# Three order changes at the seams of a two-phase float16 MLP: where eight transposing reads are issued, two gelus behind two takes, and one maximum's transpose behind a first product

## The chip, the cores and the metric

The kernel runs on one core of a Trainium2 chip. Its engines each work through a queue of their own in order: TensorE (PE, matmuls), VectorE (DVE), ScalarE (ACT), GpSimd (POOL) and SyncE (SP, which here only issues transfers). The metric is the device time of the whole program in microseconds (us). Times are medians of several runs; a profile is one execution of its own.

## The reference

Inputs are x (8 x 1024 x 1024), w1 (1024 x 4096) and w2 (4096 x 1024), all float32.

```python
h = x @ w1
h = 0.5 * h * (1 + np.tanh(np.sqrt(2 / np.pi) * (h + 0.044715 * h ** 3)))
return (h @ w2).astype(np.float32)
```

## The kernel before, in words

**Two phases.** The 8192 rows of x are cut into 32 pairs of 128-row blocks. Phase one computes gelu(x @ w1) and stores it as float16 in a DRAM tile `gd` of each pair; phase two reads `gd` back transposed and multiplies it by w2. Values are scaled into float16 by maxima that are found on the way, and both phases save matmuls by forming sums of blocks, in the manner of Strassen.

**Phase one** goes by quads. A quad `(k, r)` is pair k with quarter r of each half of the columns of w1: 256 rows, 2 x 512 columns. Class `Quad1` makes its four output blocks with seven products of four matmuls (128 x 512), in three PSUM banks: `pa` (3 buffers), `pb` (2), `pc` (3). `order` lists 128 quads (`NQ`): the first six pairs (`FIRST`) by quarters, the 22 middle pairs one by one, and the last four (`LAST`) by quarters again. The first seven quads are done plainly; from quad 7 on, `unit(u)` writes out one quad's work interleaved with what is left of quads u-1 and u-2: on PE `m1(u)`, `m7(u-1)`, `m3(u-2)`, `m2(u)`, `m6(u)`, `m5(u)`, `m4(u-1)`.

A finished block goes through ACT (a copy out of PSUM into a tile `e`, lines 503, 513, 522, and the gelu, line 454), POOL (the cast to `g`, line 177) and SP (the store to `gd`, line 459). There are 8 tiles `g`; four are written in each quad, so a cast of quad u needs the stores of two quads earlier to have landed. The stores are collected in `held` and let go at two places in each unit, always leaving the last two for the next place. Tiles `e` are freed by POOL's cast; they share a pool of 11 with the float16 sums `gs` of phase two.

**Slots.** Side work is entered into `todo` by `plan(u, slot, f, ...)` and written out by `background(u, slot)`, 0 to 6, between the products of unit u. Three kinds matter here:

- `widest_w1(r)` and `scale_w1(r)` find the largest absolute value of a quarter of w1. DVE reduces each partition and writes the result along the rows of `spread` (line 155); PE transposes `spread` into `rows` (line 162, in `all_partitions`); DVE reduces that (line 165) and derives the scales that `factors` and the casts of w1 use.
- `fetch_w2` (line 396) brings one of 25 prepared combinations of w2, 512 KB, from the DRAM tile `wd`, seven to a quarter: in quads 117 and 118, 121 and 122, 125 and 126, and four in unit 128. They use the tiles that w1's finished quarters leave.
- `load_g(k, i)` (line 550) is one transposing read of a quarter of a pair's `gd`, 512 KB, issued by SP.

**Where the phases meet.** Units 128 and 129 have no quad of their own. They finish quads 126 and 127, and twice each call `extra`, which is `second(3)`: three products of phase two. Phase two has 26 products (`PRODUCTS`) of eight matmuls (128 x 256) for each pair; each adds into the bank of one of its chains, and after a product `take` reads the bank into output blocks `o`: the first take of a block is ACT's (line 575), the later ones DVE's (line 571). A chain's next product waits until the takes of its last one have read the bank. `sum_g` (lines 168 and 171, DVE) makes the combinations of the pair's transposed blocks. Pairs 0 and 1 are read during phase one, eight reads in all; from pair 2 on four reads are issued together at the start of the pair before.

In unit 128 ACT's queue holds, in this order: the copy of `m7(127)`, quad 126's `g21` (a gelu in place in PSUM and a cast by ACT itself, line 175), the gelu `g11`, takes of products 0, 1 and 2, the gelus `g22(127)` and `g12(126)`, takes of products 3 and 5.

Of the kernel before, what the change touches and what calls it, by code (L numbers as in the profile page):

```python
# [79 lines left out]
def kernel(  # L80
# [380 lines left out]
    def let_go(n=None):  # L461
        for f in held[:n]:
            f()
        del held[:n]
# [157 lines left out]
    NQ = len(order)  # L622
    todo = {}

    def plan(u, slot, f, *args):
        assert 0 <= u, (f, args)
        todo.setdefault((u, slot), []).append((f, args))

    def background(u, slot):
        for f, args in todo.pop((u, slot), ()):  # L630
            f(*args)
# [37 lines left out]
    for r in range(2, NR):  # L669
        u = (r - 1) * FIRST - 1  # L670
        for n in range(8):
            v = u - 1 + n // 2
            if r == 2:
                plan(*((4, 1), (5, 0), (5, 2), (6, 1))[n // 2], load_w1, r, n)
                look = ((5, 3), (5, 4), (6, 1), (7, 1), (7, 1), (7, 4), (7, 5), (8, 1))[n]
                plan(*look, look_w1, r, n, S if n % 2 else V)
            else:
                plan(v, 1, load_w1, r, n)
                look = (v + 2, 1) if n == 1 else (v + 1, 3 + n % 2)
                plan(*look, look_w1, r, n, S if n == 1 else V)  # L680
        plan(u + 3, 3 if r == 2 else 5, widest_w1, r)
        plan(*((u + 3, 6) if r == 2 else (u + 4, 2)), scale_w1, r)
        plan(u + 4, 2, factors, 0, FIRST, r)
        for n in range(8):
            v, slot = ((4, 3), (4, 4), (4, 5), (5, 1), (4, 3), (4, 5), (5, 3), (4, 6))[n]
            plan(u + v, slot, cast_w1, r, n, (G, S, G, S, G, V, S, V)[n])
        for i, t in enumerate((T1, T3, T2, T4)):
            plan(u + 5 + i // 2, (4, 6, 1, 3)[i], sum_w1, r, t)
# [21 lines left out]
    u = at[middle[0]] - 1  # L710
# [8 lines left out]
    for c in range(8):  # L719
        v = u + 2 + c * 7  # L720
# [12 lines left out]
    for i, node in enumerate(FORMS):  # L733
        r, n = divmod(i, 7)
        plan(at[last[0]] + (r + 1) * LAST + (r < 3) + (n > 4), n, fetch_w2, node)
    for i in range(4):
        plan(NQ - 10 + i, 3, load_g, 0, i)
        plan(NQ - 5 + i, 3, load_g, 1, i)
    for at_, *what in LEFT_SUMS:
        if at_ < 0:  # L740
            plan(NQ - 1, 6, sum_g, 0, *what)
# [1 line left out]
    def unit(u, extra):  # L743
        q = now.get(u)
        p1, p2 = now.get(u - 1), now.pop(u - 2, None)
        if u < NQ:
            q = now[u] = Quad1(*order[u])
            q.m1()
        background(u, 0)
        if p1:  # L750
            p1.m7()
        if p2:
            p2.g21(u >= NQ)
        if p1:
            p1.g11()
        if u >= NQ:
            extra()
        let_go(len(held) - 2 if len(held) > 2 else 0)
        background(u, 1)
        if p2:  # L760
            p2.m3()
        background(u, 2)
        if u < NQ:
            q.m2()
        background(u, 3)
        if u < NQ:
            q.m6()
        if p1:
            p1.g22()
        if p2:  # L770
            p2.g12()
        let_go(len(held) - 2 if len(held) > 2 else 0)
        background(u, 4)
        if u < NQ:
            q.m5()
        background(u, 5)
        if p1:
            p1.m4()
        if u >= NQ:
            extra()  # L780
        background(u, 6)

    with tc.manual_schedule(
# [76 lines left out]
        for u in range(FIRST + 1, NQ):  # L860
            unit(u, None)
# [4 lines left out]
        for u in range(NQ, NQ + 2):  # L866
            unit(u, lambda: second(3))
# [34 lines left out]
```

## Time and profile before

| | us |
|---|---|
| median of 3 runs | 1540.9 (1540.29 to 1543.32) |
| the profiled execution, whole | 1538.59 |
| its span, first to last instruction | 1536.8 |
| PE busy in the span | 1520.7 (99%) |
| DVE, ACT, POOL busy | 1181.2, 734.6, 479.2 |
| mean granted TensorE clock | 0.999 |

The page's first part gives the busy time of each engine. The second cuts the span into 40 slices; PE shows a 7 in the first and a 9 (90% or more) in all others. In the list of groups the matmuls of phase one stand as 379 ns each (128 x 512) and those of phase two as 273 ns (128 x 256); they overlap in the pipeline, and their starts are what counts. In the timeline a quad of phase one is 28 matmuls and repeats every 6.04 us, and a pair of phase two is 208 matmuls and repeats every 22.71 us. An answer row of the timeline reads: start, duration, engine, line, operation, output and inputs, count, and in brackets the idle time before it and what ended it.

### The profile page before, as it was taken

Reading aid. Unit: us, or ns where it says so; the run is one execution under the profiler, and the core shown is the slowest. Engines: PE = TensorE matmul, PEld = TensorE weight load, DVE = VectorE, ACT = ScalarE, POOL = GpSimd, SP = SyncE. Lnnn points to the kernel's source line nnn. Section 1 sums busy time; section 2 is a strip of 40 time slices with the busy share of each in tenths; the row PEclk is TensorE's granted clock in tenths of the full one; section 3 lists DMA queues with packets and bytes.
Section 4 is the critical chain, followed back from the end, with each engine's and each line's share of the span. In section 5 each row is a group of like instructions: output and inputs, shape, how many; then the busy total and the mean of one; then the engine's idle time right before and its main releaser. Section 6 shows DMA issues by size and latency. Waiting matters only on the chain.

```text
span 1536.8 us, 28616 instructions
## 1 busy us (share of the span) xinstructions
PE 1520.7 (99%) x10398; PEld 1014.6 (66%) x10398; DVE 1181.2 (77%) x2409; ACT 734.6 (48%) x1302; POOL 479.2 (31%) x592
## 2 busy tenths in 40 slices
PE   7999999999999999999999999999999999999999
PEld 4444444444444444444448888888888888888888
DVE  6896788777877777574348888888888888888886
ACT  7778777777777777787662111111111111111111
POOL 5778554555666655554440000000000000000000
PEclk9999999999999999999999999999999999999999
DMA  9754988878788787873997668767767867866772
GB/s 351 238 189 126 299 273 292 253 233 243 211 239 269 220 260 229 246 201 103 268 258 193 132 128 154 140 134 140 148 131 135 155 136 123 165 135 124 154 141 80
DMA packets 459807, 293.94 MB, mean 191 GB/s; under 512 B 333840, under 2 KB 427024, under 8 KB 459664
## 3 DMA queue, kind: packets, MB, share of 16 engines
q1 hardware_dynamic: 456208, 279.52, 71.4%
q0 software_dynamic: 3456, 12.58, 2.6%
q8 instruction: 81, 1.33, 0.4%
q14 instruction: 62, 0.51, 0.1%
HBM read 96.99 MB, written 114.29 MB: 137 GB/s over the span
## 4 chain that ended last, share of the span: by engine, by line
PE 95%; DMA 1%; POOL 1%; ACT 1%; issue 1%; DVE 1%; SPq 0%; ACTq 0%; POOLq 0%
PE pa L402 51%; PE pc L402 30%; PE pb L402 14%; POOL g L177 1%; DMA gd<-g 1%; DMA wn<-in_w_dram 0%; ACT e L442 0%; PE pb L414 0%; POOL wn L276 0%; DMA xn<-in_x_dram 0%; ACT junk L190 0%; PE turned L216 0%; POOL w L177 0%; DVE x L179 0%; ACT xT L221 0%
## 5 line engine op out<-in xcount | busy, mean ns | idle before, releaser
L402 PEld LDWEIGHTS <-gs 128*128 128x128 f16 x4608 | 451.2, 98 | 56.4 <-issue 3.4
L177 POOL TENSOR_SCALAR g<-e,rs 128x512 f16<-128x512 f32 x446 | 364.6, 827 | 286.1 <-ACT e L454 250.0
L402 PEld LDWEIGHTS <-xs 128*128 128x128 f16 x1936 | 189.4, 98 | 227.9
L168 DVE TENSOR_TENSOR e<-pc,e 128x512 f32<-128x512 f32 x242 | 161.7, 686 | 199.9 <-ACT e L522 198.3
L402 PEld LDWEIGHTS <-xT 128*128 128x128 f16 x1676 | 163.2, 98 | 196.8 <-issue 1.7
L402 PE MATMUL pa<-w,gs 128*128 128x256 f16 x2304 | 289.0, 273 | 3.1 <-ACT o L575 3.1
L402 PE MATMUL pa<-w,xT 128*128 128x512 f16 x1080 | 256.1, 379 | 1.2 <-DVE w L179 0.9
L454 ACT ACTIVATE e<-e,us 128x512 f32<-128x512 f32 x363 | 249.2, 719 | 3.2 <-DVE e L168 3.2
L402 PE MATMUL pa<-w,xs 128*128 128x512 f16 x968 | 248.4, 379 | 0.0
L402 PE MATMUL pc<-w,xs 128*128 128x512 f16 x968 | 248.4, 379 | 0.0
L402 PEld LDWEIGHTS <-gT 128*128 128x128 f16 x2048 | 200.7, 98 | 23.6
L575 ACT ACTIVATE o<-pa,vo 128x256 f32<-128x256 f32 x96 | 45.3, 472 | 332.7 <-PE pa L402 332.7
L402 PE MATMUL pc<-w,gs 128*128 128x256 f16 x1536 | 193.8, 273 | 0.0
L402 PE MATMUL pa<-w,gT 128*128 128x256 f16 x1024 | 132.7, 273 | 0.0
L402 PE MATMUL pb<-w,xT 128*128 128x512 f16 x484 | 124.2, 379 | 0.0
L571 DVE SCALAR_TENSOR_TENSOR o<-pc,vo,o 128x256 f32<-128x256 f32 x160 | 77.1, 482 | 58.0 <-PE pc L402 58.0
L513 ACT COPY e<-pa 128x512 f32<-128x512 f32 x121 | 70.9, 586 | 91.7 <-PE pa L402 85.5
L171 DVE TENSOR_TENSOR gs<-gT,gs 128x1024 f16<-128x1024 f16 x160 | 109.3, 683 | 0.3 <-POOL g L177 0.3
L571 DVE SCALAR_TENSOR_TENSOR o<-pa,vo,o 128x256 f32<-128x256 f32 x192 | 92.3, 481 | 19.9 <-PE pa L402 19.9
L402 PE MATMUL pc<-w,gT 128*128 128x256 f16 x768 | 100.1, 274 | 0.0
L402 PE MATMUL pb<-w,gs 128*128 128x256 f16 x768 | 99.5, 273 | 0.0
L503 ACT COPY e<-pa 128x512 f32<-128x512 f32 x121 | 70.1, 579 | 50.8 <-PE pa L402 50.6
(104 smaller groups left out, 1444.8 us busy)
## 6 DMA issues: line engine op xcount, KB each, us to landing
gd<-g SPq DMA_DIRECT2D x484, 128.0 KB, 3.3
wn<-in_w_dram SPq DMA_DIRECT2D x72, 512.0 KB, 5.5
xn<-in_x_dram SPq DMA_DIRECT2D x64, 512.0 KB, 5.4
out_dram<-o SPq DMA_DIRECT2D x62, 512.0 KB, 3.5
w<-wd SPq DMA_DIRECT2D x25, 512.0 KB, 5.8
wn<-in_w_dram POOLq DMA_DIRECT2D x24, 512.0 KB, 5.9
wd<-wt SPq DMA_DIRECT2D x24, 512.0 KB, 5.0
gd<-g SPq DMA_DIRECT2D x14, 256.0 KB, 5.4
```

Of the source, the lines that this page charges most:

```text
L168: V.tensor_tensor(out=o, in0=a, in1=b, op=ALU.add)
L171: V.tensor_tensor(out=o, in0=a, in1=b, op=ALU.subtract)
L177: G.tensor_scalar(out=o, in0=i, scalar1=s, scalar2=1.0, op0=ALU.mult, op1=ALU.mult)
L402: nc.tensor.matmul(bank, lhsT=left(i), rhs=right[i], start=start and i == 0, stop=i == n - 1, skip_group_check=True,)
L454: S.activation(out=e, in_=src, func=ACT.Gelu_apprx_tanh, scale=self.u[half][s])
L503: S.copy(self.e11, self.pa)
L513: S.copy(self.e12, self.pa)
L571: V.scalar_tensor_tensor(out=o, in0=ps, scalar=v, in1=o, op0=ALU.mult, op1=ALU.add)
L575: S.activation(out=o, in_=ps, func=ACT.Copy, scale=v)
```

## The change

1. The eight transposing reads of pairs 0 and 1 move. Before, they are planned in slot 3 of units 118 to 121 and 123 to 126; after, in slot 3 of units 114, 115, 116, 119 (pair 0) and 120, 123, 124, 127 (pair 1).
2. In units 128 and 129, which have no quad of their own, the gelus `g22` and `g12` are written out at the end of the unit, behind the second call of `extra`, instead of between `m3` and `m4`. On ACT this moves two gelus (of quads 127 and 126) behind the takes of products 3 and 5; the order of DVE and PE is untouched by it.
3. `scale_w1` for quarter 2 of w1 moves from slot 6 of unit 8 to slot 0 of unit 9. On PE its one transpose stands behind the four matmuls of `m1` of quad 9 instead of ahead of them; on DVE its three small operations stand behind one more sum of x.

No operation is added or removed.

```diff
-        plan(*((u + 3, 6) if r == 2 else (u + 4, 2)), scale_w1, r)
+        plan(u + 4, 0 if r == 2 else 2, scale_w1, r)
...
-    for i in range(4):
-        plan(NQ - 10 + i, 3, load_g, 0, i)
-        plan(NQ - 5 + i, 3, load_g, 1, i)
+    for i, v in enumerate((14, 13, 12, 9, 8, 5, 4, 1)):
+        plan(NQ - v, 3, load_g, *divmod(i, 4))
...
-        if p1:
-            p1.g22()
-        if p2:
-            p2.g12()
+        def gelus():
+            if p1:
+                p1.g22()
+            if p2:
+                p2.g12()
+
+        if u < NQ:
+            gelus()
...
             p1.m4()
         if u >= NQ:
             extra()
+            gelus()
```

## The prediction, made before the changed kernel was run

> **What bounds the kernel now.** I read the page's first parts, then the waits with PE as the waiting engine, then the timeline at the places they name, then windows around them. PE is busy for 99% of the span, and outside the first 40 us only two waits lie on it:
>
> ```profile
> PE pa L402 <- ACT o L575: 3.1, 1, 3.1
> PE rows L162 <- DVE spread L155: 0.9, 1, 0.9
> ```
>
> Elsewhere phase one repeats every 6.04 us and phase two every 22.71 us, which is 28 and 208 matmul starts: nothing but these two gaps can be won, and any gain is a shift of all that follows. The windows around the first gap (busy time of PE, PEld, DVE, ACT, POOL, then granted clock, DMA share, GB/s):
>
> ```profile
> 797.79:803.86 6.07, 6.07 (x41) 3.92 (x40) 4.50 (x8) 2.36 (x4) 4.53 (x4) 1.00 1.04 226
> 803.86:807.13 3.27, 0.17 (x2) 0.00 (x1) 1.29 (x2) 1.72 (x4) 0.43 (x2) 0.90 1.02 225
> 807.13:810.36 3.23, 3.23 (x18) 2.33 (x18) 2.85 (x5) 2.37 (x5) 0.66 (x2) 0.58 0.99 353
> 810.36:833.07 22.71, 22.71 (x206) 19.99 (x205) 18.67 (x37) 5.07 (x10) 2.79 (x3) 1.00 0.49 179
> ```
>
> PE stands for 3.27 us, and behind that the granted clock is 0.58 for 3.23 us. Sixteen matmuls (products 3 and 4) start from 807.13 to 810.19, 3.06 us, where sixteen take 1.75 later. The gap thus costs 3.27 + 1.31 = 4.58 us. The chain that makes it, from the timeline:
>
> ```profile
> 789.24 6.28 SPq L550 DMA_TRANSPOSE gT<-gd  x1
> 795.61 1.00 SPq L459 DMA_DIRECT2D gd<-g  x2
> ...
> 798.17 4.00 SPq L550 DMA_TRANSPOSE gT<-gd  x1
> ...
> 802.27 1.01 SPq L459 DMA_DIRECT2D gd<-g  x2
> 805.41 0.69 ACT L175 ACTIVATE g<-pa,rs 128x512 f16<-128x512 f32 x1 [3.05 <-DMA gT<-gd]
> 806.00 0.71 ACT L454 ACTIVATE e<-e,us 128x512 f32<-128x512 f32 x1
> 806.61 0.46 ACT L575 ACTIVATE o<-pa,vo 128x256 f32<-128x256 f32 x1
> 807.13 1.86 PE L402 MATMUL pa<-w,gs 128*128 128x256 f16 x8 [3.10 <-ACT o L575]
> ```
>
> Backwards: product 3 waits for the take of product 0 (806.61), which stands on ACT behind a gelu and behind the cast at 805.41. That cast needs a tile `g`, freed when the store at 802.27 lands (3.1 us later). The store stood on SP behind a transposing read that holds the queue for 4.00 us. It belongs to slot 3 of quad 126, whose PE work began at 786.56; the cast it stores ran on POOL at 789.81. So SP is some 11 us late. The row names the read as releaser; the program's own wait is for the stores, and the first one's landing fits.
>
> Why it is late: in 741 to 801 the DMA share is 1.00 to 1.06 in every 12 us window (in 717 to 729 it is 0.26). The eight reads hold SP for 2.31 to 6.28 us, median 4.40. The two shortest (2.31, 2.45) follow four stores with no w2 fetch close before; the two longest (6.04, 6.28) follow three fetches directly.
>
> The second gap, in unit 8:
>
> ```profile
> 74.90 1.22 DVE L150 TENSOR_REDUCE w1c<-wn 128x1 f32<-128x1024 f32 x1 [0.66 <-DMA wn<-in_w_dram]
> ...
> 77.23 1.03 PE L402 MATMUL pa<-w,xT 128*128 128x512 f16 x4
> 78.77 0.29 DVE L155 TENSOR_SCALAR spread<-identity,w1a 128x128 f32<-128x128 f32 x1
> 79.11 0.33 PE L162 MATMUL rows<-identity,spread 128*128 128x128 f32 x1 [0.86 <-DVE spread L155]
> 79.28 1.03 PE L402 MATMUL pa<-w,xT 128*128 128x512 f16 x4
> ```
>
> The four matmuls of `m4` are through at 77.23 + 4 x 0.216 = 78.09; `m1` of quad 9 is ready but stands behind the transpose, which waits for `spread`, late by a transfer that landed at 74.88. The clock stays at 1.00 here.
>
> **The change, part by part.**
>
> *Transpose of quarter 2's maximum.* The DVE order up to `spread` is the same, so it is ready at 79.06 again. `m1` runs at 78.09 to 78.96, the transpose at 79.11, `m7` at 79.28 instead of 80.14: gain 0.86 us, the length of `m1`, with 0.15 of wait left. On DVE the maximum comes behind one more sum (0.41 us): scales ready at about 81.0 instead of 80.7. Their first readers run at 83.75 (`factors`) and 84.37 (POOL's cast, behind its own queue), so this is hidden by some 2.7 us; without that cover it would cost 0.4. Bounds 0.3 (the transfer lands earlier) to 0.86.
>
> *Reads moved.* Work of the DMA engines, from windows: 717 to 729 moves eight stores at share 0.26, so 0.39 us a store; a pair of phase two (four reads, two 512 KB outputs, about 0.65 of 22.7 us, the outputs 1.5 us each at the stores' rate) gives 2.9 us a read; 741 to 801 (about 14 fetches, 7.5 reads, 36 stores) leaves 1.86 us a fetch. Before, quads 117 up to the late store ask for 21 x 1.86 + 8 x 2.9 + 42 x 0.39 = 78.6 us, and took from 732.3 to about 805.4, 73.1: the estimate is 7% high. After, three of the reads lie in quads 114 to 116 where the share is 0.26; up to the same store of quad 126 there are 19 fetches, 4 reads, 40 stores: 62.5, scaled 58.2 us, from 732.3 that is 790.5, about when its cast is done. SP's own time agrees: in a quad with a read 4 stores (0.5 each) + 2.3 to 4.4 against 6.04; in one with five fetches (0.45 each) 4.3. So the store goes out near 790.5 to 791, not 802.3, and lands, at 3.3 to the longest 7.2 us seen there, by 798.2. ACT's cast would want it at 800.9: copy at 799.77 (end of `m7` 799.51 plus the 0.26 seen in every quad), gelu 0.48 later, cast 0.69 later. Gelu 801.5, take of product 0 at 802.1 to 802.6; product 3 may start at 803.86. Margin 1.2 us. The gap goes with its slow clock: gain 4.58.
>
> What is late next? The last read (quad 127) starts near 794.3, ends by 798.7 (4.4) or 800.6 (6.3), and holds the stores behind it; the first is wanted by ACT's cast of `g21(127)` in unit 129, at about 809. Even at 7.2 to landing it is there by 808.3. Behind that cast stands the take of product 7, wanted by product 12 at 812.6.
>
> DVE becomes the next tight one: the sum for product 6 (node 25) ends a row that starts at 800.9 (sums without a break from 797.0, then `vo` and `vn`, 0.8): 800.9 + 0.6 (add) + 3 x 0.65 (sums) + 0.4 (take) + 0.65 (add) + 1.4 (two sums) = 805.9, wanted at 806.48. Bounds for the reads: 1 us (a shorter gap with the slow clock left) to 4.58.
>
> *Gelus later.* In unit 128 as it now runs, both orders have the take of product 3 in time: with the gelus ahead, 803.9 (product 2's second take, behind DVE's) + 0.46 + 2 x 0.66 + 0.46 = 806.1 against 806.48; behind, 805.45. Value 0 here; it turns 0.4 us of cover into 1.0. Put behind, the gelus wait for product 5 (806.5 + 0.3) and end at 808.4; POOL's casts follow at 808.6 to 810, and DVE's next sum that needs a freed tile comes at 809.9. Bounds -0.5 to +0.5 if that sum waits, or if the cover would have been gone.
>
> **Sum.** 0.86 + 4.58 + 0 = 5.44 us. The profiled execution then reads 1538.59 - 5.4 = 1533.2, span 1531.4. The median of the runs shown is 2.3 us above the profiled one; I take the same gain from it: 1540.9 - 5.4 = 1535.5.
>
> One page speaks against the largest term. The Trainium skill, "Advanced Engine Details and Errata", section "X-Bar Transpose (TRN2)", states that transpose DMAs are as fast as regular ones; by it a read would be no worse a neighbour than a fetch, moving it would free little, and the result would be that of rival B. The trace disagrees: fetches of the same 512 KB hold SP for 0.32 to 1.03 us here.
>
> **Rivals.**
>
> A. *The lag only shrinks.* 7 fetches, 2 reads and 16 stores in four quads ask for 25 us (unscaled) of 24.2, so the DMA engines stay nearly full from 117 on, and the read in 127 follows two fetches. If half of the 3.27 us is left, gain 0.86 + 1.6 (clock slow again) to 0.86 + 2.95 (not): 1537.1 to 1538.4. For: shares above 1.0 without a break. Against: three reads and the last one are out of the way.
>
> B. *The reads cost what other transfers cost,* or something else frees the tile `g` late, so that the gap stays: only 0.86 is won, 1540.0. For: the row that names a read as releaser. Against: the 11 us lag of SP.
>
> C. *The last read turns against its neighbours* (slower). It sits in quad 127 instead of 126, directly ahead of the last stores, fetches and ACT's in-order queue. If it is held so long that its store lands after 811.4 (812.58 less 1.15 for cast and take), product 12 stands, one for one, and from a gap near 3.3 us also 1.3 for the clock. That needs the read to hold SP past 803, against a longest of 6.28 us from 794.3. With the old gap still there and 3.3 + 1.3 added, less 0.86: 1544.6. For: the reads before do just that. Against: the 2.5 us of slack with the longest rows.
>
> That the change does nothing is B without the first term; the changed kernel's order of instructions shows all three moves.
>
> **How the numbers follow.** Forecast (gap gone, 1533.5 to 1537) 0.69; A 0.16; B 0.10; C 0.05. A measurement of this kernel tells about 0.2% (3.1 us) from no change, so faster means under 1537.8. The forecast and about half of A are that: 0.77. B and half of A: 0.18. C: 0.05. The range reaches from 1533.0 (the ordinary runs, slower than the profiled one, may have had a longer gap) to 1539.6, which takes in A and part of B.
>
> **What would show it.** Right: no wait of PE for ACT's takes; m4 of quad 127 followed at once by product 3; clock 1.00 there; reads of 114 to 116 at about 2.4 us on SP; at the meeting SP within 3 us of POOL's casts; `m1` of quad 9 ahead of the transpose. Wrong: POOL waiting for stores in 790 to 800 again, or a new PE wait for a sum of DVE at product 6.

## The result, and the profile after

| | before | after |
|---|---|---|
| median of the runs | 1539.8 us (1538.73 to 1543.32, 6 runs) | 1534.68 us (1533.26 to 1535.61, 6 runs) |
| ratio | | 0.9957, 95% interval 0.9946 to 0.9967 |
| profiled execution, whole / span | 1538.59 / 1536.8 us | 1534.61 / 1532.8 us |

The changed kernel is faster by 0.33 to 0.54%, the interval of the ratio. The two medians differ by 5.1 us, 0.33%, which is its lower end. 1535.5 us had been forecast. First the longest waits of PE in the profile of the changed kernel (engine and line, what it waited for, then microseconds in total, times, longest):

```profile
PE turned L216 <- ACT x L175: 7.2, 1, 7.2
PE rows L162 <- DVE spread L155: 1.0, 1, 1.0
```

The first of them lies in the first 8 us and is the same before (7.1). The wait for ACT's take, 3.1 us before, is not in the list. The wait for `spread` is, and it is longer than before (0.86). Where the phases meet, the windows of the changed kernel (busy time of PE, PEld, DVE, ACT, POOL, then clock, DMA share, GB/s) read:

```profile
799.11:804.32 5.21, 5.21 (x38) 3.52 (x37) 5.17 (x9) 3.52 (x7) 3.78 (x3) 1.00 1.01 265
804.32:806.06 1.74, 1.74 (x17) 1.57 (x16) 1.74 (x4) 0.84 (x2) 0.00 (x0) 1.00 0.93 309
806.06:828.90 22.84, 22.84 (x207) 19.88 (x205) 19.64 (x39) 6.11 (x12) 2.58 (x3) 1.00 0.36 124
```

PE is busy through, products 3 and 4 take 1.74 us instead of 3.06, and the clock stays at 1.00. The DMA share there is still about 1. SP and ACT, from the same timeline:

```profile
787.63 4.36 SPq L459 DMA_DIRECT2D gd<-g  x4
...
794.77 4.22 SPq L550 DMA_TRANSPOSE gT<-gd  x1
799.09 1.01 SPq L459 DMA_DIRECT2D gd<-g  x2
```

```profile
801.41 0.69 ACT L175 ACTIVATE g<-pa,rs 128x512 f16<-128x512 f32 x1
802.00 0.71 ACT L454 ACTIVATE e<-e,us 128x512 f32<-128x512 f32 x1
802.61 0.46 ACT L575 ACTIVATE o<-pa,vo 128x256 f32<-128x256 f32 x1
```

The four stores from 787.63 are those of quad 126's first and second place; the last two of them are the ones that went out at 802.27 before. They now wait only for POOL's two casts (from 790.27, 0.69 us each), and the first of them goes out at 790.99. ACT's cast at 801.41 has no idle time in brackets, and the take of product 0 is through 1.2 us before product 3 may start (804.32).

The span fell by 4.0 us, not by the 5.4 of the sum. The missing 1.4 us lie in three places. The first has nothing to do with the change: 0.34 us are lost within the first 14 us of this execution (the first product starts at 13.73 instead of 13.39), and so `m4` of quad 7 starts at 77.57 instead of 77.23. The second is unit 8 (rows of DVE and PE):

```profile
75.53 1.22 DVE L150 TENSOR_REDUCE w1c<-wn 128x1 f32<-128x1024 f32 x1 [0.93 <-DMA wn<-in_w_dram]
76.66 0.84 DVE L168 TENSOR_TENSOR xs<-xT 128x512 f16<-128x512 f16 x1
77.57 1.89 PE L402 MATMUL pa<-w,xT 128*128 128x512 f16 x8
79.81 0.57 DVE L155 TENSOR_SCALAR spread<-identity,w1a 128x128 f32<-128x128 f32 x1
80.43 0.33 PE L162 MATMUL rows<-identity,spread 128*128 128x128 f32 x1 [0.97 <-DVE spread L155]
80.60 1.03 PE L402 MATMUL pa<-w,xs 128*128 128x512 f16 x4
```

`m1` of quad 9 does run ahead of the transpose here: it is the second half of the eight matmuls from 77.57. But `spread` was ready 1.3 us later than in the profile before (80.38 instead of 79.06). Of this, 0.6 us are the transfer, which landed later and with it the reduction; 0.7 are two operations of DVE that took longer in this execution, a sum of x (0.84 us, 0.41 before) and the write of `spread` (0.57, 0.29 before). What made them longer is not shown. From the end of `m4` to the start of `m7`, less the four matmuls of `m1`, it is 1.30 us, and 1.18 in the profile before: 0.12 lost where 0.86 was to be won. The third is product 6:

```profile
805.60 1.40 DVE L171 TENSOR_TENSOR gs<-gs 128x1024 f16<-128x1024 f16 x2
806.06 2.05 PE L402 MATMUL pa<-w,gs 128*128 128x256 f16 x16
807.95 1.91 PE L402 MATMUL pc<-w,gs 128*128 128x256 f16 x16
```

From 806.06 to 807.95 are 1.89 us for sixteen starts that take 1.75: 0.14 for a sum of DVE, which ends at 807.00 where product 6 could have started at 806.93. 0.34 + 0.86 + 0.12 + 0.14 is the 1.46 that is missing.

### The profile page after: what moved, and what is told of

The parts are those of the page before. It is cut to its first block, busy times and chain, and to the rows that moved or that the text cites. A ratio compares the mean times of both kernels' runs of the same rounds, so it can differ in the third digit from the quotient of the medians.

```text
span 1532.8 us, 28623 instructions
## 1 busy us (share of the span) xinstructions
PE 1519.6 (99%) x10398; PEld 1014.1 (66%) x10398; DVE 1183.0 (77%) x2409; ACT 734.5 (48%) x1302; POOL 479.6 (31%) x592
## 4 chain that ended last, share of the span: by engine, by line
PE 95%; DMA 1%; POOL 1%; ACT 1%; DVE 1%; issue 0%; ACTq 0%; POOLq 0%
PE pa L402 51%; PE pc L402 30%; PE pb L402 14%; DMA gd<-g 1%; POOL g L177 1%; DMA wn<-in_w_dram 0%; ACT e L442 0%; PE pb L414 0%; POOL wn L276 0%; DMA xn<-in_x_dram 0%; ACT junk L190 0%; PE turned L216 0%; POOL w L177 0%; DVE x L179 0%; ACT xT L221 0%
```

## The experiments

### Each part alone

Three kernels carry one part of the change each, with the lines of the diff in the section on the change; the fourth carries the first and the third part.

> Only the eight reads move. Queue theory (the gap where the phases meet comes from SP standing behind transposing reads, so that stores free the tiles g late): the 3.3 us gap and its slow clock go; left may be a short wait of PE for the take of product 3, which stands behind two gelus again (about 0.4 us). 3.9 to 4.6 us faster than before, some 1535.5 us. Rival (ACT's order makes the gap: gelus ahead of takes): the gap stays near 3 us and the time within 1 us of before.

> Only the transpose of quarter 2's maximum moves behind m1 of quad 9. Queue theory: the gap where the phases meet stays at 3 us or more; on its own the move hides up to 0.86 us (the length of m1) of the wait for spread, whenever that wait is longer than that, so 0.3 to 0.9 us faster, 1539.0 to 1539.5 us. Rival (the wait moves with whatever PE does, because DVE's work ahead of spread follows PE): nothing, within 0.2 us, and the wait of PE for spread as long as before, about 0.9 us.

> Only the two gelus move behind the takes of products 3 and 5. Queue theory: the cast that waits for a store stands ahead of both on ACT, so the gap stays at 3 us or more and the time within 0.5 us of before, 1539.5 to 1540. Rival (ACT's order makes the gap): 2 us or more faster, with the gap shorter than 1.5 us.

> The change without its gelu part. Queue theory: as the whole change but for the take of product 3 behind two gelus: by the changed kernel's rows it would end at about 807.3 us where product 6 could start at 806.9, so 0.3 to 0.6 us slower than the whole change, about 1535.1 us, and a wait of PE for an ACT take of that size. If the gelu part is worth nothing (as forecast): the same as the whole change within 0.2 us. Rival (ACT's order makes the gap): 2 us or more slower than the whole change.

| run | median | before, same chip | ratio, 95% interval | gap ahead of product 3 |
|---|---|---|---|---|
| reads alone | 1534.52 us | 1540.59 us | 0.9960 (0.9948 to 0.9973) | none |
| transpose alone | 1540.38 us | 1540.59 us | 0.9999 (0.9990 to 1.0008) | 4.2 us |
| gelus alone | 1541.29 us | 1540.59 us | 1.0005 (0.9996 to 1.0014) | 3.5 us |
| reads and transpose | 1534.01 us | 1540.59 us | 0.9961 (0.9948 to 0.9975) | none |

The gap column is PE's wait for ACT's take. With the reads alone moved, product 3 follows `m4` of quad 127 at once:

```profile
803.50 1.03 PE L402 MATMUL pa<-w,xT 128*128 128x512 f16 x4
804.36 1.04 PE L402 MATMUL pa<-w,gs 128*128 128x256 f16 x8
```

The reads do what the whole change does. By the medians they win 6.1 us, and the interval leaves 4.2 to 8.0 us, so the 3.9 to 4.6 expected were at the low end. The other two parts show nothing in the times: the transpose alone, expected 0.3 to 0.9 us faster, came out 0.2 us faster, with an interval from 1.5 us faster to 1.2 slower (its rival forecast such a time, but for a wait for `spread` as long as before, and none is left in its profile); the gelus alone, expected within 0.5 us of before, came out 0.7 us slower, with no change inside the interval. In the two runs that leave the reads where they were, the gap was longer than the 3.1 us of the profile before: that profile had one of the shorter ones. With the transpose alone moved, PE also waited 0.9 us ahead of product 2, for a sum of DVE that waited for POOL, whose cast had waited 7.0 us for stores. The rival, by which ACT's order makes the gap, falls: with the gelus alone moved, ACT's cast waits as it did.

```profile
802.72 0.67 ACT L454 ACTIVATE pa<-pa,us 128x512 f32<-128x512 f32 x1
806.73 0.69 ACT L175 ACTIVATE g<-pa,rs 128x512 f16<-128x512 f32 x1 [3.34 <-DMA gT<-gd]
807.32 0.71 ACT L454 ACTIVATE e<-e,us 128x512 f32<-128x512 f32 x1
807.93 0.46 ACT L575 ACTIVATE o<-pa,vo 128x256 f32<-128x256 f32 x1
```

The gelus that moved stand behind all of this, and so cannot shorten it.

What the gelu part is worth once the reads are out of the way shows in the fourth run, in its rows of ACT and PE:

```profile
804.11 1.32 ACT L454 ACTIVATE e<-e,us 128x512 f32<-128x512 f32 x2
805.34 0.46 ACT L575 ACTIVATE o<-pa,vo 128x256 f32<-128x256 f32 x1
```

```profile
804.69 2.20 PE L402 MATMUL pa<-w,gs 128*128 128x256 f16 x16
806.72 1.91 PE L402 MATMUL pc<-w,gs 128*128 128x256 f16 x16
```

With the two gelus ahead, the take of product 3 is through at 805.80, and product 6 could have started at 805.56. From 804.69 to 806.72 are 2.03 us for sixteen starts, 0.28 more than 1.75; in the whole change it is 0.14, and there DVE's sum is the later one. The same holds in every profile with early reads: 2.02 or 2.03 us with the gelus ahead (reads alone, reads and transpose, and the early reads further down), 1.88 or 1.89 with them behind (the change twice, slot 2 twice). The gelu part thus saves some 0.14 us, less than expected here (0.3 to 0.6), and far below what the times can tell.

### How much later may the transpose go?

Slot 2 of unit 9 instead of slot 0, on top of the whole change, run twice; the second time beside the changed kernel itself.

```diff
-        plan(u + 4, 0 if r == 2 else 2, scale_w1, r)
+        plan(u + 4, 2, scale_w1, r)
```

> The whole change, with the transpose of quarter 2's maximum two places later still (slot 2 of unit 9, behind m1, m7 and m3, as the other quarters have it). If the wait for spread is set by a transfer that lands when it will (74.3 to 76.8 us in the profiles so far, spread done at 78.5 to 80.4), no wait of PE is left there in any execution: 0 to 1.1 us faster than the whole change, about 1534.0 us, span near 1531.4. Rival (scales become late for the casts of w1 and PE waits for those): a new wait of PE for DVE's, POOL's or ACT's w, and 0.5 us or more slower than the change.

> The changed kernel once more, beside the next run on the same chip: 1534.0 to 1535.0 us. Its wait for spread changes from execution to execution with the transfer that lands at 74 to 77 us.

> The change with the transpose in slot 2 of unit 9, beside the changed kernel on the same chip. If the wait for spread that is left in the change is worth something: 0.4 to 0.9 us faster than the change, 1533.8 us, with a smaller spread of its runs. If it is not: within 0.3 us of it.

Measured: 1533.83 us, ratio to before 0.9956 (0.9944 to 0.9969); on the second chip 1534.00 us beside 1533.91 us for the changed kernel, which is just below the 1534.0 to 1535.0 expected of it. The times don't tell the two apart, and so no version is shown to beat the change. The profiles say more than the times, because the cost can be read in each: from the end of `m4(7)`, as its start plus four matmuls, to the start of `m7(8)`, less the four matmuls of `m1`. In the seven profiles with the transpose ahead of `m1` (before, reads alone, gelus alone, and the four runs further down) this is 0.43 to 2.25 us, on average 1.07; in the four with it in slot 0 it is 0.10, 0.11, 0.11 and, in the profile shown above, 1.30, on average 0.41; in the two with slot 2 it is nothing, and the transpose itself takes its 0.11 two products later. So the move is worth about 0.7 us in these few profiles. The same comes out as an estimate from each of the seven alone, as the part of its wait that the 0.86 us of `m1` would have covered: 0.3 to 0.86, on average 0.7. Slot 2 takes away what is left when `spread` is late. With differences of 1 us and more between executions, medians of five runs can't confirm it.

### What makes the store late: fetches beside the reads, their sum, or their order?

Four kernels keep the transpose and the gelus as before and change only where reads or stores are issued. The reads doubled in quiet quads:

```diff
-        plan(NQ - 10 + i, 3, load_g, 0, i)
-        plan(NQ - 5 + i, 3, load_g, 1, i)
+    for i, v in enumerate((9, 9, 8, 8, 5, 5, 4, 1)):
+        plan(NQ - v, 3, load_g, *divmod(i, 4))
```

The early reads, some in busy quads (114 to 117, 119 to 121 and 126, of which 117, 121 and 126 have fetches), differ from this by the list alone:

```diff
-    for i, v in enumerate((9, 9, 8, 8, 5, 5, 4, 1)):
+    for i, v in enumerate((14, 13, 12, 11, 9, 8, 7, 2)):
```

The stores of quads 124 to 126 on ACT, and the reads behind the stores, against the kernel before:

```diff
-            held.append(lambda: nc.sync.dma_start(out=o, in_=g))
+            queue = S if self.r == NR - 1 and NP - LAST <= self.k < NP - 1 else nc.sync
+            held.append(lambda: queue.dma_start(out=o, in_=g))
```

```diff
-        plan(NQ - 10 + i, 3, load_g, 0, i)
-        plan(NQ - 5 + i, 3, load_g, 1, i)
+        plan(NQ - 10 + i, 4, load_g, 0, i)
+        plan(NQ - 5 + i, 4, load_g, 1, i)
```

> The reads alone move, all in quads without fetches but seven of them ahead of the late store and inside the stretch of the fetches: two each in quads 119, 120, 123, one each in 124 and 127. Load theory (the DMA engines are asked for more than they can do between quad 117 and the meeting): 19 fetches, 7 reads and 40 stores ask for 66 us from 732.3 (same scale as in the prediction), so the store of g21(126) goes out near 798 and lands at 802 to 805, where 802.2 is wanted: a gap of 0 to 3 us, 1534.5 to 1539. Neighbour theory (a read is only slow on SP where fetches stand close before it): reads hold SP for 2 to 3 us, no gap, as fast as reads alone in the change, 1534.5.

> The reads alone move, seven of them as early as in the change or earlier but three of those into quads with fetches (114, 115, 116, 117, 119, 120, 121), the last one stays in 126, which has fetches. Load theory: five reads after 732.3 instead of eight: 61 us asked for, the late store goes out near 793 to 796 and lands by 800: no gap, 1534.5 us, though single reads hold SP for 4 to 6 us. Neighbour theory (each read behind fetches holds SP for 4 to 6 us and so do these): a part of the gap is left, 1 us or more, 1536 to 1539.

| run | median | before, same chip | ratio, 95% interval |
|---|---|---|---|
| reads doubled in quiet quads | 1535.09 us | 1540.56 us | 0.9964 (0.9950 to 0.9977) |
| early, some in busy quads | 1534.61 us | 1540.56 us | 0.9962 (0.9948 to 0.9975) |

The reads of the second run, from its timeline on SP, quads 117, 121 and 126:

```profile
737.01 6.34 SPq L550 DMA_TRANSPOSE gT<-gd  x1
...
766.33 5.64 SPq L550 DMA_TRANSPOSE gT<-gd  x1
...
792.30 5.50 SPq L550 DMA_TRANSPOSE gT<-gd  x1
```

In the quads with fetches (117, 121 and 126) the reads hold SP for 5.5 to 6.3 us, as long as the longest before, and in 119, which has none, for 5.5, and yet PE has no gap at product 3. A quad without fetches is thus not what is needed. In the first run all reads stand in quads without fetches, but seven of them in the crowded stretch; they hold SP for 1.9 to 4.6 us each (median 3.7), and the last, planned for quad 127, goes out at 801.68 where it does at 794.77 in the changed kernel. SP is 7 us late, and a gap is back, though a smaller one and at product 6:

```profile
805.61 1.04 PE L402 MATMUL pa<-w,gs 128*128 128x256 f16 x8
807.96 1.03 PE L402 MATMUL pa<-w,gs 128*128 128x256 f16 x8 [1.31 <-ACT o L575]
808.83 1.91 PE L402 MATMUL pc<-w,gs 128*128 128x256 f16 x16
```

```profile
801.80 3.09 POOL L177 TENSOR_SCALAR g<-e,rs 128x512 f16<-128x512 f32 x3 [1.14 <-DMA gd<-g]
803.72 0.69 DVE L171 TENSOR_TENSOR gs<-gT 128x1024 f16<-128x1024 f16 x1 [0.51 <-POOL g L177]
```

So what is asked for in the crowded stretch decides how late SP is, as the load theory has it. That the 1.3 us lie within its 0 to 3 is partly luck, for it meant the gap at product 3. There the store went out at 796.13 and the cast ran in time, at 802.15. The gap that came took another path: POOL's casts waited for stores, sums of DVE for POOL (0.33 and 0.51 us), and the takes of products 2 and 3 came late behind them. What the three quiet quads 114 to 116 are worth is that they lie ahead of the crowded stretch.

Two accounts of the lateness are not told apart by these runs: the work that the DMA engines are asked for, and the time for which the reads hold SP's own queue. Every run that takes reads out of the stretch lowers both.

> The kernel before, reads as before, but ACT issues the stores of quads 124, 125 and 126 (12 issues), so that they do not stand behind the reads on SP. Queue theory (the store is late because it stands behind reads in SP's queue): the cast in unit 128 no longer waits, the 3.3 us gap goes or shrinks below 1 us; 2 to 4.5 us faster than before if ACT's issues (0.4 us each) hide, 1535.5 to 1538. Rival (the DMA engines are so full that the store lands late from whichever queue it is issued): the gap stays at 2 us or more.

This one failed as an experiment: 1544.06 us, ratio 1.0020 (1.0009 to 1.0031), slower. The stores on ACT brought waits of their own:

```profile
801.98 0.82 ACTq L460 DMA_DIRECT2D gd<-g  x2
802.89 0.59 ACT L504 COPY e<-pa 128x512 f32<-128x512 f32 x1 [6.67 <-DMA gT<-gd]
```

In the program's list of instructions every transfer of SP and ACT waits for the one eight issues back, by one of eight semaphores that the two share; the store that ACT was to issue waited for a read that was still under way, and all of ACT's queue with it, and for ACT PE's `m7`, 5.74 us. SP follows the same rule in every kernel here, but it is not what made SP late: in the profile before, SP's waits for a landing add up to only 2.0 us from 730 to 806. Whether the store would have landed early from an undisturbed queue is not answered by this run.

> The kernel before, with its reads in the same eight quads but in slot 4 instead of 3, which puts each one behind the two stores of its quad on SP instead of ahead of them; the same transfers in the same stretch. Queue theory (what matters is how much stands ahead of the store in SP's queue): the store of g21(126) goes out one read earlier, near 798 instead of 802.3, lands at 801 to 802.5, where 802.2 is wanted: the 3.3 us gap shrinks to 0 to 1.5 us, without the slow clock, 1535 to 1537. Rival (the DMA engines are so full that the store lands late anyway): a gap of 2 us or more and the time within 1.5 us of before.

The last kernel answers it for a store that goes out 1 us earlier. Its time is within what was called no gain, 1541.61 us against 1540.15, ratio 1.0007 (0.9998 to 1.0016), but not for the rival's reason, which has the store late as before. Its SP, ACT and PE:

```profile
794.08 6.02 SPq L550 DMA_TRANSPOSE gT<-gd  x1
800.19 1.98 SPq L459 DMA_DIRECT2D gd<-g  x4
802.26 2.04 SPq L550 DMA_TRANSPOSE gT<-gd  x1
804.35 1.05 SPq L396 DMA_DIRECT2D w<-wd  x2
805.50 3.14 SPq L459 DMA_DIRECT2D gd<-g  x4
```

```profile
803.51 0.69 ACT L175 ACTIVATE g<-pa,rs 128x512 f16<-128x512 f32 x1 [2.26 <-DMA gd<-g]
```

```profile
805.22 1.03 PE L402 MATMUL pa<-w,gs 128*128 128x256 f16 x8 [1.78 <-ACT o L575]
...
808.49 1.03 PE L402 MATMUL pa<-w,gs 128*128 128x256 f16 x8 [0.49 <-ACT o L575]
...
815.01 1.89 PE L402 MATMUL pc<-w,gs 128*128 128x256 f16 x8 [4.61 <-DVE gs L171]
```

```profile
813.06 1.36 POOL L177 TENSOR_SCALAR g<-e,rs 128x512 f16<-128x512 f32 x2 [6.63 <-DMA gd<-g]
```

The two stores that stood behind the read at 798.17 before are now the last two of the four from 800.19. They go out about 1 us earlier, the cast runs at 803.51 instead of 805.41, and the gap at product 3 shrinks from 3.10 to 1.78 us (PE itself is 0.6 us earlier in this execution). But the read has only changed places with them. The next stores stand behind it and go out from 805.50, 1.15 us later than before, and the first takes 7.4 us to land where it took 5.6; so there the fullness that the rival names has its part. POOL's cast waits for them (6.63 us in its row at 813.06), a sum of DVE waits for POOL to free a tile, and product 8 waits 4.61 us for the sum. SP is as late as it was; the order decides which store pays, and which wait PE gets. PE's gaps became smaller as a whole only where less was asked for ahead of the meeting: in the change and its parts with the reads, in the reads doubled and in the early reads.

## Why the prediction was right, point by point

- *What bounds the kernel.* Right: the gaps of PE are all that moved, and their changes add up to the change of the span (4.0 us).
- *The chain of the first gap,* a store behind reads on SP, a cast waiting for a tile `g`, the take of product 0 behind it: shown by reads alone (gap gone) and by gelus alone (gap kept). That the store, not the read the row names, releases the cast at 805.41 shows in the landings of the profile before: the read issued at 798.17 landed 6.3 us later, at 804.5, the store issued at 802.27 landed 2.9 us later, at 805.2. In the reads behind the stores the same wait is put down to `gd<-g`.
- *Reads moved,* 4.58 us. Right in every step that was timed, with PE 0.46 us later in this execution: store out when its cast is done (forecast 790.5 to 791, 790.99 measured), cast wanted at 800.9 (801.41 measured), take of product 0 at 802.1 (802.61), last read near 794.3 (794.77) for 4.4 us (4.22). Reads in quiet quads were to hold SP for 2.4 us: 2.37, 2.81 and 1.32. In the ordinary runs the term is larger: reads alone won 6.1 us by the medians (4.2 to 8.0), and the two other profiles with the reads in their old place have gaps of 3.5 and 4.2 us.
- *The scaled sum of transfers,* 58 us asked for up to the late store, was good enough to place that store. For the reads doubled (66 us) it put the store near 798, and it went out at 796.13; the 1.3 us of gap found there came by another path than the one it was meant for.
- *Transpose of the maximum,* 0.86 us. The step that was meant, `m1` running during the wait, is there in the rows; the size depends on when `spread` is ready, and that differs from execution to execution. The lower bound was given as 0.3 from an early landing, while in the profile of the changed kernel the transfer landed late, two operations of DVE took longer, and the wait was 0.12 us longer than in the other profile. That an execution in which `spread` comes later still would eat the term was left out of the bounds. Over the profiles it is worth about 0.7; the times show nothing (0.9999).
- *The sum.* 1535.5 us was forecast and 1534.68 measured, and this closeness is partly luck: the reads won more in the ordinary runs than their 4.58 us, and the transpose, in the one pair of profiles that the sum was made for, won nothing of its 0.86.
- *Gelus later,* 0. Right within what can be measured. But the cover named for it was not there: the take of product 3 with the gelus ahead was put 0.4 us ahead of its need, and it came 0.24 us behind it, since DVE's sums and with them product 2's second take ran 0.7 us later than their rows added up to. The part is worth 0.14 us, not cover alone.
- *What is late next.* DVE's sum for product 6, named as the next tight one with 0.6 us to spare, did come to set it, by 0.14 us. Such a wait stood among the signs of being wrong; at this size it is only a small miss of the sum. The other sign, POOL waiting for stores between 790 and 800, appears in one row (792.95) that names a store, but its 1.32 us of idle are those of the quads in which ACT is the releaser. The last read in quad 127 did no harm.
- *The rivals.* A and B did not come. Against B the prediction set how long SP is held, which is not how fast a transfer is: to landing the eight reads of the profile before took 6.3 to 8.3 us (median 7.1) and the fetches 3.6 to 7.3 (5.8), a smaller difference than that of the holds. C did not come in the change, but what it describes, stores behind the last reads making a later product wait, is what the reads behind the stores show (4.61 us at product 8).

## What to carry to other kernels

When an engine stands for a buffer that a store must free, follow the store back into the queue that issues it and add up what that queue and the transfer engines are asked for from where the crowding begins; a lateness of 11 us had built up over ten quads and showed on PE only where the slack between phases ran out. Here, moving work ahead of the crowded stretch removed the lateness, while swapping neighbours in the queue, in the one try made, only handed it to the next waiter. A wait that depends on a landing time has to be judged over several profiles: one pair showed a loss of 0.12 us where the thirteen together show a gain of about 0.7. And a shift between two profiles has to be followed back to where it begins: 0.34 of the 0.46 us by which PE was late behind unit 8 had been lost in the first 14 us.

## What the runs showed of the hardware that was not expected

- The granted clock did not fall behind every gap of PE. After waits of 1.31, 1.78 and 1.92 us (reads doubled, reads behind the stores, and the wait for `spread` in the early reads) it was 1.00; with waits of 3.10, 3.47, 4.19, 4.61 and 5.74 us (before, gelus alone, transpose alone, reads behind the stores, stores on ACT) it went to 0.50. The 0.58 of the prediction is the mean of a window that reaches into full speed again. The clock went down while PE still stood, 2.3 to 5.2 us after its last matmul, and stayed at 0.50 for 3.41 us in four of the five profiles and for 6.83, twice as long, in the reads behind the stores. First the profile before, then that one:

```profile
806.46:809.87 3.41, 2.74 (x14) 1.89 (x14) 2.36 (x5) 2.86 (x7) 0.69 (x1) 0.50 0.91 305
812.68:819.51 6.83, 4.50 (x18) 2.61 (x19) 4.33 (x7) 1.30 (x3) 1.36 (x2) 0.50 0.88 259
```

  So the length of a gap does not by itself say when the clock falls. What does was not tried.

- A transposing read of 512 KB held SP's queue for anything from 1.32 us (quad 116 of the changed kernel, with a DMA share of 0.41) to 7.78 us (quad 125 of the transpose alone, behind three fetches), while a plain fetch of the same size held it for 0.32 to 1.03 us in the profile before. What sets the time between these ends was not tried apart from the crowding.
